# The 64-row and 32-row matmuls of two heads take turns, one by one, instead of head after head

## The chip, the cores and the metric

The kernel runs on one core of a Trainium2 chip. The metric is the device time of one launch in microseconds; three runs of the kernel before took 4888.07, 4894.80 and 4915.18 us, and their median, 4894.8 us, is the time before.

## What is computed

Two inputs of 1024 tokens by 1024 channels (a prompt and a sample) each go through two encoder layers, so there are four units of work. A layer is an input projection, four mixers side by side, and an output projection:

```
h = rms_norm(x, g_pre) * (1 + scale) + shift
proj = h @ w_in                                # 1024 x 1024 by 1024 x 3800
o_a = mla_mixer(...)                           # softmax attention, 4 heads
o_b = rwkv7_mixer(...)                         # linear attention with decay, 2 directions, 4 heads
o_c = mamba2_mixer(...)                        # state space, 2 directions
o_d = gated_deltanet_mixer(...)                # delta rule, 2 directions, 4 heads
x + gate * rms_norm(concat(o_a, o_b, o_c, o_d) @ w_out, g_post)
```

Mixers B and D are recurrences over the tokens. They are worked in 16 chunks of 64 tokens. Within a chunk a unit triangular 64 x 64 system is solved; between chunks a 64 x 64 state per head is carried. All of it is fp32.

## The kernel before

**Two heads lie in the two halves of the partitions.** A head has 64 channels and a chunk has 64 tokens, so in mixers B and D one head of a pair stands in partitions 0 to 63 and the other in 64 to 127. The code calls the half `x` (or `h`), the pair `pr`, and `half(x)` is the slice of 64 partitions. A matmul of one head reads 64 partitions and writes 64 partitions of PSUM, so it uses one 64 x 64 quarter of the TensorE array; a 32 x 32 matmul uses one sixteenth. Every fp32 matmul stands in the trace as two weight loads and two matmul records.

**Chunk matrices of mixer B** (`rwkv_dir`, lines 814 to 828). For each of 2 halves, 2 pairs and 16 chunks, two matmuls (`a` = 0, 1) read the rows of half `x` and write the two halves of PSUM in turn (line 824). Four chunks fill a bank of 512 columns; three banks (`b2p`) take turns. VectorE evicts a bank in four instructions (line 828). The loop over `x` is the outermost.

**Inverses** (`invert`, `merge`, lines 515 to 559). VectorE inverts the 32 x 32 diagonal blocks; `merge` joins them into 64 x 64 inverses with two rounds of 32 x 32 matmuls, for two groups `g` of 16 chunks. The round on line 551 fills one bank for each half `h`, ScalarE copies it to `Qs` (line 552), the round on line 558 multiplies `Qs` again, and VectorE copies the result (line 559). For each half there are 16 matmuls and then the half's copy. Three banks take turns, two a round. `merge` runs 16 times: 4 units, 2 mixers, 2 directions.

**The chains** (`rwkv_chain`, `gdn_chain`). 16 chunks in order, each a few small matmuls with VectorE and ScalarE between them (lines 905, 915, 928, 931 in B; 1195, 1207, 1220 in D). Those loops already have the half `x` innermost. Once for two chunks `batch` prepares the next pair: in B it loads `UV` by two DMAs, one for each half, then 8 matmuls (line 863) and 8 flips by the identity (line 565, called from 866) fill one PSUM tile `w`, ScalarE copies it, and 8 matmuls (line 875) fill another; in D it is 8 matmuls (line 1177). In all three the loop over `x` is the outermost. There are 64 batches of each mixer (4 units, 2 directions, 8 pairs of chunks).

**The order of the work.** A unit's mixers run in two streams (D then A; B then C) beside the projections of the neighbouring units: `in_tile` and `out_tiles` issue bulk 128 x 128 matmuls on line 458 through `paced`, whose groups of 5 or 8 are released by a memset on GpSimd (line 462). A planner writes every engine's queue ahead of time from the priorities given in the program: `urgent` puts `merge`, the chains and the weight splits (lines 327 and 329) ahead of the bulk. On the chip each engine then takes its queue in that fixed order, and an instruction that waits for a semaphore holds what is queued behind it.

Of the kernel before, what the change touches and what calls it, by code (L numbers as in the profile page):

```python
# [18 lines left out]
DRAM = bass.MemoryType.DRAM  # L19
MUL, ADD, SUB = ALU.mult, ALU.add, ALU.subtract  # L20

D = 1024
# [86 lines left out]
class Body:  # L109
# [22 lines left out]
    def open_io(self, ctx):  # L132
        """the pools of the projections"""
        self.pj = self.pool(ctx, "pj")
        self.sp = self.pool(ctx, "sp", 2)
        self.pps = self.pool(ctx, "pps", 2, PSUM)
# [20 lines left out]
    def sumsq(self, ps, col, sq, n, rhs, w, start=True, stop=True):  # L157
        """ps[:, col:col+w] = per-token sums over the channels of sq[:, 128 n : 128 n + 128]"""
        for x in range(2):
            self.nc.tensor.matmul(ps[64 * x:64 * x + 64, col:col + w], sq[:, n * 128 + 64 * x:n * 128 + 64 * x + 64], rhs,  # L160
                                  start=start, stop=stop)
# [99 lines left out]
    def stage_in(self, s, L, l, xsrc, Pd, parts=((0, W_ORDER), (1, W_ORDER))):  # L261
        """parts: (token half, tiles); the half of the part before is still there"""
        for hf, names in parts:
            if self.held is None or self.held[0] != (Pd, hf):
                self.spread()
                hh = self.t(self.pj, [128, 8, 512], F32R, tag="hh")
                hl = self.t(self.pj, [128, 8, 512], F32R, tag="hl")
                self.norm_in(s, L, xsrc, hf, hh, hl)
                self.held = (Pd, hf), hh, hl
            for name in names:  # L270
                self.spread()
                self.in_tile(l, name, hf, *self.held[1:], Pd)
# [59 lines left out]
    def out_tiles(self, l, ch, hh, hl, kqs, at=lambda kq: kq):  # L332
        """products of 4 token tiles with a quarter of the columns of w_out, over the quarters kqs of its rows"""
        nc, pj = self.nc, self.pj
        pss = [self.t(self.pps, [128, 2, 256], tag="pj") for _ in range(2)]
        for n, kq in enumerate(kqs):
            w = self.t(pj, [128, 2, 256], tag="w", bufs=2)
            self.dma(w, self.A["w_out"][l, ch, kq // 2][:, (kq % 2) * 512:(kq % 2) * 512 + 512].rearrange("p (k c) -> p k c", k=2))
            with self.urgent():
                wh, wl = self.split_w(w, [128, 2, 256])  # L340
            for i in range(4):
                ps = pss[i // 2][:, i % 2]
                c = slice(i * 128, (i + 1) * 128)
                for k in range(2):
                    a, b = hh[:, at(kq) * 2 + k, c], hl[:, at(kq) * 2 + k, c]
                    first, last = n == 0 and k == 0 and i % 2 == 0, n == len(kqs) - 1 and k == 1
                    for m, (u, w2) in enumerate(((a, wh), (a, wl), (b, wh))):
                        self.paced(TO, ps, u, w2[:, k], dict(start=first and m == 0, stop=last and m == 2, skip_group_check=True))
        return pss
# [50 lines left out]
    def stage_out_last(self, s, L, l, xsrc, od, dst, parts, ctx=None):  # L400
        """the last output in parts (token half, quarters of the rows of w_out, whether the sums begin or end),
        while the mixers of the later quarters still run"""
# [53 lines left out]
    def paced(self, n, *mm):  # L456
        """a matmul of a bulk stream: groups of n, each issued after the group before has begun"""
        m = self.nc.tensor.matmul(*mm[:3], **mm[3]).ins  # L458
        if self.gate is not None:
            self.tc.add_manual_dep(m, self.gate[0], SYNC, reason="pace")  # L460
        if self.run == 0:
            t = self.nc.gpsimd.memset(self.token, 0.0).ins  # L462
            self.tc.add_manual_dep(t, m.name, SYNC, reason="pace")
            self.next = t.name
        self.run += 1
        if self.run == n:
            self.gate, self.run = (self.next,), 0

# [10 lines left out]
    def behind(self, p0, p1, n, fs):  # L479
        """emit fs with priorities spread over those from p0 to p1"""  # L480
        keep = self.tc.cur_priority
        self.span, self.step = (p0, p1, n), 0
        for f in fs:
            f()
        self.span = None
        self.tc.cur_priority = max(keep, p1)
# [28 lines left out]
    def invert(self, pool, r, d, src):  # L515
        """r = inverses of the unit triangular 32 x 32 diagonal blocks of src, transposed"""
# [15 lines left out]
    def merge(self, pool, psp, r, d, src, dst):  # L532
        """dst = inverse of the unit triangular 64 x 64 blocks of src from the inverses r of their diagonal blocks"""
# [9 lines left out]
        for g in range(2):  # L543
            gs = slice(g * 16, g * 16 + 16)
            Qs = self.t(pool, [128, 16, 32], tag="mQ")
            p1 = [self.t(psp, [128, 512], tag="b") for _ in range(2)]
            for h in range(2):
                pa, pb = 64 * h + a, 64 * h + b
                A, B = slice(pa, pa + 32), slice(pb, pb + 32)
                for i in range(16):  # L550
                    nc.tensor.matmul(p1[h][B, i * 32:i * 32 + 32], src[h][a:a + 32, g * 16 + i, b:b + 32], Tr[A, g * 16 + i, :], start=True, stop=True, tile_position=(pa, pb))  # L551
                nc.scalar.copy(Qs[B].rearrange("p i t -> p (i t)"), p1[h][B])
            p2 = [self.t(psp, [128, 512], tag="b") for _ in range(2)]
            for h in range(2):
                pa, pb = 64 * h + a, 64 * h + b
                A, B = slice(pa, pa + 32), slice(pb, pb + 32)
                for i in range(16):
                    nc.tensor.matmul(p2[h][A, i * 32:i * 32 + 32], Qs[B, i, :], dst[h][b:b + 32, g * 16 + i, b:b + 32], start=True, stop=True, tile_position=(pb, pa))  # L558
                nc.vector.tensor_copy(dst[h][a:a + 32, gs, b:b + 32], p2[h][A].rearrange("p (i t) -> p i t", t=32))
# [7 lines left out]
    def pair_t(self, psp, dst, src, scale=None):  # L567
        """dst[(c parity, t), (c // 2, x, e)] = transposes of 8 chunks of both heads of src, times scale[(c parity, t), c // 2, x]"""
# [9 lines left out]
    def dma_pair(self, dst, src, swap):  # L578
        """dst[(x or 1 - x, t), c, e] (DRAM) = src[(c parity, t), (c // 2, x, e)]"""
# [6 lines left out]
    def head_sum(self, ps, sq, n):  # L586
        """ps[half, i] = sums over the channels of the head of the other half"""
# [4 lines left out]
    def heads_back(self, psp, y):  # L592
        """transposes back to channels: y[(1 - x, t), c, pr, e] -> [(pr, e), x, c, t]"""
# [5 lines left out]
    def rows2(self, t, r0, q):  # L599
        """rows r0 to r0 + 256 and quarter q of the tokens"""  # L600
# [55 lines left out]
    def rwkv_norm(self, p, psp, L, Pd, q, y, yd, bon, od, free):  # L656
        """normalisation, bonus and gate of a quarter of the tokens"""
# [29 lines left out]
    def rwkv_dir(self, L, Pd, l, d, yds, bons, od):  # L687
        nc, v = self.nc, self.nc.vector
        yd, bon = yds[d], bons[d]
        with ExitStack() as c0:  # L690
# [124 lines left out]
            with ExitStack() as c1:  # L815
                psp = self.pool(c1, "b2p", 3, PSUM)
                for x in range(2):
                    for pr in range(2):
                        for c4 in range(4):
                            ps = self.bank(psp)  # L820
                            for i in range(4):
                                c = c4 * 4 + i
                                for a in range(2):
                                    nc.tensor.matmul(ps[self.half(x ^ a), i * 128:i * 128 + 128], BK[self.half(x), pr, c, a],  # L824
                                                     AR[self.half(x), pr, c].rearrange("p a t -> p (a t)"), start=True, stop=True)
                            for i in range(4):
                                c = c4 * 4 + i
                                v.scalar_tensor_tensor(G[:, x, pr, c, :], ps[:, i * 128:i * 128 + 128], Dk[:, c, 2 * x + pr:2 * x + pr + 1], mk, MUL, MUL)  # L828
# [17 lines left out]
    def rwkv_chain(self, p, psp, d, AR, G, PL, Dk, vd, bkd, yd, pn, finish):  # L846
# [4 lines left out]
        def batch(j):  # L851
# [8 lines left out]
            for x in X:  # L860
                for pr in X:
                    for i in X:
                        nc.tensor.matmul(ps[half(1 - x), (pr * 2 + i) * 64:(pr * 2 + i) * 64 + 64], G[half(x), x, pr, 2 * j + i, 0:64], UV[half(x), x, pr, i, :],  # L863
                                         start=True, stop=True)
                        o = 256 + (pr * 2 + i) * 64
# [6 lines left out]
            for x in X:  # L872
                for pr in X:
                    for i in X:
# [199 lines left out]
    def gdn_norm(self, p, psp, L, Pd, q, y, yd, fq, od, free):  # L1074
        """normalisation and gate of a quarter of the tokens"""
# [70 lines left out]
    def gdn_chain(self, p, psp, d, GT, SC, kvd, be, kds, neg, el, yd, pn, finish):  # L1146
# [16 lines left out]
        def batch(j):  # L1163
# [10 lines left out]
            for x in X:  # L1174
                for pr in X:
                    for i in X:
# [321 lines left out]
    def attend(self, p, psp, qd, kd, krd, VO, ot):  # L1498
        """softmax of every head; the maxima of a head are found during the head before"""
# [74 lines left out]
    def mixers(self, L, Pd, l, od, which="dcab"):  # L1574
        """the streams right (d, a) and left (b, c)"""
# [9 lines left out]
    def last_mixers(self, L, Pd, l, od, io):  # L1585
        """three streams: d, c on the right; b; a in the place of the projections"""
# [16 lines left out]
    def full(self):  # L1603
# [32 lines left out]
        def ahead(w, n, f):  # L1636
            """emit f with priorities spread over the next w, n steps"""
# [87 lines left out]
```

## Time and profile before

| | |
|---|---|
| median of three runs | 4894.8 us |
| span of the profiled execution | 4894.9 us |
| PE (TensorE matmul) busy | 4389.3 us, 90% |
| DVE (VectorE) busy | 3343.1 us, 68% |
| ACT (ScalarE) busy | 2178.9 us, 45% |
| POOL (GpSimd) busy | 397.6 us, 8% |
| mean granted TensorE clock | 0.878 of full speed |

The span runs from the first to the last instruction; with one core there is nothing around it that the time would hold besides, and the two differ by 0.1 us. A busy time is the union of an engine's instructions. Matmul records last longer than the spacing of their starts, since matmuls are pipelined; what a run of matmuls costs is read from the start of its first to the start of the next thing behind it.

### The profile page before, as it was taken

To read this page: it belongs to the slowest core of one execution; us is meant where nothing else is said; L and a number is where in the kernel's file an instruction comes from. 1 tells how busy PE (TensorE), PEld (TensorE's weight loads), DVE (VectorE), ACT (ScalarE), POOL (GpSimd) and SP (SyncE) were. 2 spreads that over 40 slices of the span, in tenths; PEclk is the share of its full clock that TensorE was granted. 3 is DMA by queue.
4 is the path that set the end of the run, shared out by engine and by line. 5 is a ranking of instruction groups with operands and counts; after the bars stand their busy time and mean duration, and the time that the engine had idled before them with its cause. 6 is when DMAs were issued, how large, how long until landed. Compare 5 with 4: busy or idle time off the path is not lost.

```text
span 4894.9 us, 100724 instructions
## 1 busy us (share of the span) xinstructions
PE 4389.3 (90%) x38644; PEld 3358.2 (69%) x38644; DVE 3343.1 (68%) x6837; ACT 2178.9 (45%) x4734; POOL 397.6 (8%) x2093
## 2 busy tenths in 40 slices
PE   6879798999997988999989898899989989898997
PEld 3667576766776776756767667776767766776686
DVE  2488877566578787566459778657546968856666
ACT  2444363563434534443454453455344354344333
POOL 0101010000101000000011100000011100000001
PEclk8889898998997987989989798798889979878788
DMA  4444264242453546363345353545145535455224
GB/s 144 136 148 138 99 192 132 87 131 99 135 171 126 160 127 192 109 197 110 112 154 162 109 174 117 174 139 147 63 133 165 163 111 158 130 181 156 85 86 137
DMA packets 495063, 671.79 MB, mean 137 GB/s; under 512 B 149752, under 2 KB 265976, under 8 KB 493560
## 3 DMA queue, kind: packets, MB, share of 16 engines
q1 hardware_dynamic: 494584, 665.36, 43.6%
q8 instruction: 306, 5.01, 0.4%
q14 instruction: 173, 1.42, 0.1%
HBM read 486.53 MB, written 178.57 MB: 136 GB/s over the span
## 4 chain that ended last, share of the span: by engine, by line
PE 49%; DVE 13%; DMA 10%; issue 3%; ACT 3%; SPq 1%; POOL 0%; DVEq 0%; POOLq 0%; ACTq 0%
PE pj L458 21%; PE b L824 3%; PE b L1568 2%; PE b L551 2%; DVE iA L522 1%; PE b L558 1%; SPq L144 1%; PE b L1456 1%; PE b L1555 1%; PE pj L243 1%; PE w L863 1%; DVE wl L329 1%; DVE GT L537 1%; PE b L1524 1%; PE y L1220 1%
## 5 line engine op out<-in xcount | busy, mean ns | idle before, releaser
L458 PE MATMUL pj<-hh,wl 128*128 128x512 f32 (+1 forms) x2048 | 848.2, 415 | 32.0 <-DVE wl L329 18.4
L458 PE MATMUL pj<-hh,wh 128*128 128x512 f32 (+1 forms) x2048 | 854.6, 418 | 11.9 <-DVE iT L529 3.2
L458 PE MATMUL pj<-hl,wh 128*128 128x512 f32 (+1 forms) x2048 | 849.7, 415 | 16.9 <-POOL token L462 16.6
L327 ACT CAST wh<-w 128x512 fp32r<-128x512 f32 x640 | 395.1, 618 | 775.4 <-PE pj L458 495.1
L329 DVE TENSOR_TENSOR wl<-w,wh 128x512 fp32r<-128x512 f32 x640 | 446.6, 699 | 245.3 <-ACT wh L327 211.8
L458 PEld LDWEIGHTS pj<-hh,wl 128*128 128x128 f32 (+1 forms) x2048 | 397.5, 194 | 137.5 <-issue 20.7
L458 PEld LDWEIGHTS pj<-hh,wh 128*128 128x128 f32 (+1 forms) x2048 | 397.6, 194 | 115.3 <-issue 19.9
L458 PEld LDWEIGHTS pj<-hl,wh 128*128 128x128 f32 (+1 forms) x2048 | 396.9, 194 | 113.0 <-POOL token L462 22.9
L462 POOL MEMSET token<- 1x1 f32 x1613 | 143.7, 89 | 3317.1 <-PE pj L458 3307.1
L458 PE MATMUL pj<-wh,hl 128*128 128x256 f32 x896 | 266.6, 310 | 0.7 <-DVE hl L363 0.5
L458 PE MATMUL pj<-wh,hh 128*128 128x256 f32 x768 | 238.7, 311 | 6.3 <-ACT hh L362 4.1
L1559 ACT ACTIVATE pT<-b 128x512 f32<-128x512 f32 x256 | 149.8, 596 | 210.6 <-PE b L1557 207.4
L458 PE MATMUL pj<-wl,hh 128*128 128x256 f32 x768 | 234.0, 305 | 0.0
L294 PE MATMUL pj<-c_ident,x 128*128 128x128 f32 x416 | 118.8, 388 | 109.9 <-ACT hh L298 41.0
L1525 DVE TENSOR_REDUCE mx<-b 128x1 f32<-128x512 f32 x256 | 169.7, 686 | 68.5 <-PE b L1524 66.8
L638 DVE SCALAR_TENSOR_TENSOR cva<-cvi,cw,cva 128x1024 f32<-128x1024 f32 x144 | 183.9, 1279 | 47.4 <-ACT cva L634 29.3
L458 PEld LDWEIGHTS pj<-wh,hl 128*128 128x128 f32 x896 | 181.3, 207 | 14.2 <-issue 6.2
L296 ACT ACTIVATE ht<-pj,shc,gsc 128x256 f32<-128x256 f32 x208 | 118.4, 569 | 156.6 <-PE pj L294 84.0
L828 DVE SCALAR_TENSOR_TENSOR G<-b,Dk,mk 128x128 f32<-128x128 f32 x512 | 143.8, 344 | 61.9 <-PE b L824 61.1
L1568 PEld LDWEIGHTS b<-VO,pT 128*64 128x64 f32 x4096 | 150.2, 151 | 42.6 <-issue 29.4
L824 PE MATMUL b<-AR,BK 64*64 64x128 f32 x2048 | 176.7, 299 | 0.0
L1568 PE MATMUL b<-VO,pT 128*64 128x65 f32 x4096 | 168.4, 238 | 4.7 <-ACT pT L1559 4.3
(403 smaller groups left out, 9407.1 us busy)
## 6 DMA issues: line engine op xcount, KB each, us to landing
w<-w_in SPq DMA_DIRECT2D x512, 256.0 KB
P<-st SPq DMA_DIRECT2D x248, 256.0 KB
x<-x SPq DMA_DIRECT2D x76, 512.0 KB
w<-w_out SPq DMA_DIRECT2D x128, 256.0 KB
G<-P SPq DMA_DIRECT2D x112, 256.5 KB
cvi<-P SPq DMA_DIRECT2D x48, 512.0 KB
f<-acr SPq DMA_DIRECT2D x32, 512.0 KB
bkc<-bkd SPq DMA_DIRECT2D x64, 256.0 KB
```

Source lines behind the costliest of these rows:

```text
L294: nc.tensor.transpose(ps[:, i * 128:(i + 1) * 128], xs[i][:, k * 128:(k + 1) * 128], self.ident)
L296: nc.scalar.activation(ht, ps[:, 0:256], AF.Identity, scale=L.gsc[:, k, s:s + 1], bias=L.shc[:, k, s:s + 1])
L327: nc.scalar.copy(wh, w)
L329: nc.vector.tensor_tensor(wl, w, wh.bitcast(F32), SUB)
L458: m = self.nc.tensor.matmul(*mm[:3], **mm[3]).ins
L462: t = self.nc.gpsimd.memset(self.token, 0.0).ins
L638: nc.vector.scalar_tensor_tensor(a, c[:, j:j + 1024], wt(j, i), a, MUL, ADD)
L824: nc.tensor.matmul(ps[self.half(x ^ a), i * 128:i * 128 + 128], BK[self.half(x), pr, c, a], AR[self.half(x), pr, c].rearrange("p a t -> p ...
L828: v.scalar_tensor_tensor(G[:, x, pr, c, :], ps[:, i * 128:i * 128 + 128], Dk[:, c, 2 * x + pr:2 * x + pr + 1], mk, MUL, MUL)
L1525: v.tensor_reduce(mx[:, n, qt:qt + 1], ps, AX.X, ALU.max, negate=True)
L1559: nc.scalar.activation(pT[kt], ps, AF.Exp)
L1568: nc.tensor.matmul(po[64 * x:64 * x + 64, i, :], pT[kt][:, o:o + 64], VO[:, kt, h, :], start=(kt == 0 and i == 0), stop=(kt == 7), skip_gr ...
```

## The change

Four places get the half of the partitions as their innermost loop. In `rwkv_dir` a pair of banks, one for each half, is filled together and evicted afterwards. In `merge` both halves' 32 matmuls are issued in turn, and both copies come after them, in both rounds. In the three `batch` loops nothing but the order of the matmuls changes. The number of instructions, their shapes, operands and targets stay the same. (Elsewhere the diff only drops comments.)

```
@@ merge
-            for h in range(2):
-                pa, pb = 64 * h + a, 64 * h + b
-                A, B = slice(pa, pa + 32), slice(pb, pb + 32)
-                for i in range(16):
-                    nc.tensor.matmul(p1[h][B, i * 32:i * 32 + 32], src[h][a:a + 32, g * 16 + i, b:b + 32], Tr[A, g * 16 + i, :], start=True, stop=True, tile_position=(pa, pb))
+            at = [(64 * h + a, 64 * h + b) for h in range(2)]
+            AB = [(slice(pa, pa + 32), slice(pb, pb + 32)) for pa, pb in at]
+            for i in range(16):
+                for h, (A, B) in enumerate(AB):
+                    nc.tensor.matmul(p1[h][B, i * 32:i * 32 + 32], src[h][a:a + 32, g * 16 + i, b:b + 32], Tr[A, g * 16 + i, :], start=True, stop=True, tile_position=at[h])
+            for h, (A, B) in enumerate(AB):
                 nc.scalar.copy(Qs[B].rearrange("p i t -> p (i t)"), p1[h][B])
...
+            for i in range(16):
+                for h, (A, B) in enumerate(AB):
+                    nc.tensor.matmul(p2[h][A, i * 32:i * 32 + 32], Qs[B, i, :], dst[h][b:b + 32, g * 16 + i, b:b + 32], start=True, stop=True, tile_position=at[h][::-1])
+            for h, (A, B) in enumerate(AB):
                 nc.vector.tensor_copy(dst[h][a:a + 32, gs, b:b + 32], p2[h][A].rearrange("p (i t) -> p i t", t=32))
@@ rwkv_dir
-                for x in range(2):
-                    for pr in range(2):
-                        for c4 in range(4):
-                            ps = self.bank(psp)
...
+                for pr in range(2):
+                    for c4 in range(4):
+                        pss = [self.bank(psp) for _ in range(2)]
+                        for i in range(4):
+                            c = c4 * 4 + i
+                            for a in range(2):
+                                for x in range(2):
+                                    nc.tensor.matmul(pss[x][self.half(x ^ a), i * 128:i * 128 + 128], BK[self.half(x), pr, c, a],
+                                                     AR[self.half(x), pr, c].rearrange("p a t -> p (a t)"), start=True, stop=True)
+                        for x in range(2):
                             for i in range(4):
                                 c = c4 * 4 + i
...
+                                v.scalar_tensor_tensor(G[:, x, pr, c, :], pss[x][:, i * 128:i * 128 + 128], Dk[:, c, 2 * x + pr:2 * x + pr + 1], mk, MUL, MUL)
@@ rwkv_chain, batch
-            for x in X:
-                for pr in X:
-                    for i in X:
+            for pr in X:
+                for i in X:
+                    for x in X:
                         nc.tensor.matmul(ps[half(1 - x), (pr * 2 + i) * 64:(pr * 2 + i) * 64 + 64], G[half(x), x, pr, 2 * j + i, 0:64], UV[half(x), x, pr, i, :],
                                          start=True, stop=True)
+                    for x in X:
                         o = 256 + (pr * 2 + i) * 64
                         self.flip(ps[half(1 - x), o:o + 64], AR[half(x), pr, 2 * j + i, 0, :], half(x))
@@ the same turn of the loops (pr, i, x for x, pr, i) at line 875 of rwkv_chain and at line 1177 of gdn_chain
```

## Rows read from the trace of the kernel before

**Rows 1.** The page: busy times, and the chain of waits by engine.

```profile
PE 4389.3 (90%) x38644; PEld 3358.2 (69%) x38644; DVE 3343.1 (68%) x6837; ACT 2178.9 (45%) x4734; POOL 397.6 (8%) x2093
PE 49%; DVE 13%; DMA 10%; issue 3%; ACT 3%; SPq 1%; POOL 0%; DVEq 0%; POOLq 0%; ACTq 0%
```

**Rows 2.** Span and mean granted TensorE clock.

```profile
core 0: 4894.9 us, clock 0.878
```

**Rows 3.** Groups by line: operands, count, busy us, mean ns, idle before and releasers.

```profile
L824 PE MATMUL b<-AR,BK 64*64 64x128 f32 x2048 | 176.7, 299 | 0.0
...
L863 PE MATMUL w<-UV,G 64*64 64x64 f32 x1024 | 132.9, 240 | 5.6 <-DMA UV<-vd 5.0 <-DVE qf L1516 0.3 <-PE us L905 0.3
...
L552 ACT COPY mQ<-b 32x512 f32<-32x512 f32 x64 | 36.9, 576 | 228.0 <-PE b L551 228.0
...
L559 DVE COPY G<-b 32x512 f32<-32x512 f32 x32 | 22.0, 687 | 48.3 <-PE b L558 48.2
```

**Rows 4.** Timeline of a batch of B and what follows (start us, us, instruction, records).

```profile
871.58 0.32 PE L863 MATMUL w<-UV,G 64*64 64x64 f32 x2
...
873.20 0.28 PE L565 MATMUL w<-c_ident,AR 64*64 64x64 f32 x2
873.41 0.33 PE L931 MATMUL y<-UV,G 128*64 128x64 f32 x2
...
877.49 0.96 PE L875 MATMUL w<-G,At 64*64 64x64 f32 x16
878.38 0.50 PE L1524 MATMUL b<-kh,qh 96*128 96x512 f32 x1
```

**Rows 5.** Timeline of a batch of D and what follows.

```profile
434.41 0.96 PE L1177 MATMUL w<-GT,SC 64*64 64x64 f32 x16
435.30 0.50 PE L458 MATMUL pj<-hl,wh 128*128 128x512 f32 x1
```

**Rows 6.** Timeline of two runs whose halves already take turns, same stretch.

```profile
879.52 0.45 PE L905 MATMUL us<-ZS,G 128*64 128x64 f32 x8
879.90 0.44 PE L928 MATMUL y<-ZS,AR 64*64 64x64 f32 x6
880.27 0.50 PE L1524 MATMUL b<-kh,qh 96*128 96x512 f32 x1
```

**Rows 7.** Timeline of a merge alone on PE.

```profile
1897.98 3.68 PE L551 MATMUL b<-mT,G 32*32 32x32 f32 x61 [5.61 <-DVE mT L542]
...
1901.47 0.24 PE L551 MATMUL b<-mT,G 32*32 32x32 f32 x1
1901.50 0.24 PE L558 MATMUL b<-G,mQ 32*32 32x32 f32 x1
...
1910.87 0.58 PE L458 MATMUL pj<-wh,hh 128*128 128x256 f32 x1
```

**Rows 8.** Timeline of a merge at full clock, one run.

```profile
3484.50 2.01 PE L558 MATMUL b<-G,mQ 32*32 32x32 f32 x61
```

**Rows 9.** Two merges' stretches: busy us of PE, PEld, DVE, ACT, POOL; granted clock; DMA.

```profile
1898.00:1912.00 14.00, 13.98 (x261) 13.78 (x262) 10.66 (x17) 3.98 (x6) 2.10 (x4) 0.50 0.58 189
3096.90:3117.50 20.60, 20.60 (x312) 19.55 (x313) 10.42 (x19) 5.83 (x14) 0.79 (x7) 0.67 0.34 112
```

**Rows 10.** Timeline of chunk matrices, and of a run that turns both rows and columns.

```profile
737.62 1.96 PE L824 MATMUL b<-AR,BK 64*64 64x128 f32 x32
...
262.67 2.87 PE L1064 MATMUL b<-KQ 64*64 64x128 f32 x46
```

**Rows 11.** Timeline of the eviction of one bank of chunk matrices on VectorE.

```profile
742.04 1.13 DVE L828 SCALAR_TENSOR_TENSOR G<-b,Dk,mk 128x128 f32<-128x128 f32 x4 [0.18 <-PE b L824]
```

**Rows 12.** Two stretches of chunk matrices, same columns as rows 9.

```profile
735.40:761.50 26.10, 26.10 (x321) 20.48 (x321) 22.41 (x77) 2.79 (x6) 3.12 (x9) 1.00 0.27 89
2971.00:3007.70 36.70, 36.70 (x481) 30.54 (x480) 30.33 (x93) 10.61 (x31) 0.98 (x7) 0.84 0.33 104
```

**Rows 13.** Timeline of SP's queue: issue of the two loads of UV.

```profile
884.88 1.18 SPq L144 DMA_DIRECT2D UV<-vd  x2
```

More of the change, by code (lines that the diff above doesn't have):

```diff
@@ L546, in merge @@
             p1 = [self.t(psp, [128, 512], tag="b") for _ in range(2)]
-            for h in range(2):
-                pa, pb = 64 * h + a, 64 * h + b
-                A, B = slice(pa, pa + 32), slice(pb, pb + 32)
-                for i in range(16):
-                    nc.tensor.matmul(p1[h][B, i * 32:i * 32 + 32], src[h][a:a + 32, g * 16 + i, b:b + 32], Tr[A, g * 16 + i, :], start=True, stop=True, tile_position=(pa, pb))
+            at = [(64 * h + a, 64 * h + b) for h in range(2)]
[4 more added lines that the diff above has]
+            for h, (A, B) in enumerate(AB):
                 nc.scalar.copy(Qs[B].rearrange("p i t -> p (i t)"), p1[h][B])
             p2 = [self.t(psp, [128, 512], tag="b") for _ in range(2)]
[L554 to L558, printed above, removed]
+            for i in range(16):
+                for h, (A, B) in enumerate(AB):
+                    nc.tensor.matmul(p2[h][A, i * 32:i * 32 + 32], Qs[B, i, :], dst[h][b:b + 32, g * 16 + i, b:b + 32], start=True, stop=True, tile_position=at[h][::-1])
+            for h, (A, B) in enumerate(AB):
                 nc.vector.tensor_copy(dst[h][a:a + 32, gs, b:b + 32], p2[h][A].rearrange("p (i t) -> p i t", t=32))
@@ L816, in rwkv_dir @@
                 psp = self.pool(c1, "b2p", 3, PSUM)
-                for x in range(2):
-                    for pr in range(2):
-                        for c4 in range(4):
-                            ps = self.bank(psp)
+                for pr in range(2):
[8 more added lines that the diff above has]
+                        for x in range(2):
                             for i in range(4):
                                 c = c4 * 4 + i
[L823 to L828, printed above, removed]
+                                v.scalar_tensor_tensor(G[:, x, pr, c, :], pss[x][:, i * 128:i * 128 + 128], Dk[:, c, 2 * x + pr:2 * x + pr + 1], mk, MUL, MUL)
             cB.close()
@@ L871, in batch @@
             ps = self.t(psp, [128, 512], tag="w")
-            for x in X:
-                for pr in X:
-                    for i in X:
+            for pr in X:
+                for i in X:
+                    for x in X:
                         nc.tensor.matmul(ps[half(x), (pr * 2 + i) * 64:(pr * 2 + i) * 64 + 64], At[half(1 - x), pr, i, :], G[half(1 - x), x, pr, 2 * j + i, 0:64],
@@ L1173, in batch @@
             ps = self.t(psp, [128, 512], tag="w")
-            for x in X:
-                for pr in X:
-                    for i in X:
+            for pr in X:
+                for i in X:
+                    for x in X:
                         nc.tensor.matmul(ps[half(x), (pr * 2 + i) * 64:(pr * 2 + i) * 64 + 64], kn[half(1 - x), pr, i, :], GT[half(1 - x), x, pr, 2 * j + i, 0, :],
```

## The prediction

> **What bounds the kernel now.** I read the page's busy times first: TensorE is at work for 4389.3 of 4894.9 us, far more than VectorE's 3343.1 [rows 1]. The profiled execution stands at the median of the runs (4894.9 against 4894.8), so its span can be used as it is [rows 2]. The chain of waits tempers that: its PE share is 49% of the span, with 13% VectorE and 10% DMA between [rows 1]. So TensorE is the bound, but only 49 of its 90 points lie on the path that sets the end; I carry a saved microsecond of TensorE to the end at 49/90 = 0.54, and at 0.9 (its busy share) in the best case. The groups by line give the operands and counts of the lines touched; the rest is read from timelines, because there a run of matmuls has a price: from its start to the start of what stands behind it.
>
> **The rate of one array tile, and of two.** A batch of B holds 16 matmuls, 32 records, and takes 871.58 to 873.41, 1.83 us, 57 ns a record [rows 4]; all of one half use one tile of the array. Where the halves already take turns, 8 records go from 879.52 to 879.90, 0.38 us [rows 6]. With 0.24 us for one record [rows 3] inside the 0.45 us of that run, 7 steps take 0.21 us: 30 ns a record and 0.14 us at the ends. Two tiles thus run side by side, each at its old rate, and that is the whole effect of the change: where one tile was busy, two will be.
>
> **Batches.** 1.83 us becomes 0.14 + 32 x 0.030 = 1.10, so 0.73 us goes, 64 times: 47 us. The runs on line 875 (877.49 to 878.38, 0.89 us for 16 records [rows 4]) and line 1177 (434.41 to 435.30, also 0.89 us [rows 5]) become 0.14 + 16 x 0.030 = 0.62; 0.27 us, 128 times: 35 us. Nothing is added to any queue. One wait moves: the second matmul now reads the second half of `UV`. SP issues both loads in 1.18 us [rows 13], so it may come 0.6 us later, and formerly eight matmuls and eight flips of the first half covered that. At 64 batches this is 0 to 38 us; TensorE stood 5.0 us in all for `UV` in the whole run [rows 3], so the loads are mostly long there, and I take 5 us. Behind the waiting matmul stands the bulk stream, in the same queue.
>
> The Trainium skill ("TensorEngine Tiling (Array Packing)", "Gotcha 1: PSUM Pressure") says that different row tiles cannot use one PSUM bank at the same time. Both halves of a batch write one bank, so by that rule these 82 us would be nothing. Lines 905 and 928 write both halves into one bank too, 928 from different rows, and stay at 0.45 us for 8 and 0.44 us for 6 records [rows 6]; by that row I keep the 82 us and hold the rule as a rival.
>
> **Merges.** A merge alone takes 1897.98 to 1910.87, 12.9 us for 256 records, 50 ns each [rows 7], at half the clock (0.50 in that stretch, TensorE busy for 14.0 of its 14.0 us [rows 9]) after 5.61 us of standing [rows 7]. Where the end of one round overlaps the next, records of the two lines start 27 to 30 ns apart (1901.47, 1901.50) [rows 7]: two tiles, half the price. Taking turns, a round of 64 records costs 64 x 0.027 = 1.7 us, four of them 6.9. But a cover goes. Today ScalarE copies half 0 while half 1 is multiplied, and TensorE never stands in that merge. Now both copies follow the round: 0.24 us for the last record and 2 x 0.576 [rows 3] = 1.4 us, twice; and before round 3 the first VectorE copy, 0.24 + 0.687 [rows 3] = 0.9 us, because the three banks are then short by one. That is 3.7 us, so 10.6 with nothing in the gaps, and 0.69 for the second copy at the end: 1.6 us gained; 6.0 if bulk matmuls fill the gaps. A part of the merges is warmer (0.67 in one stretch [rows 9]); at full clock one tile gives (2.01 - 0.24) / 60 = 30 ns a record [rows 8], which makes 7.7 us before and, even at 15 ns, 3.9 + 3.7 + 0.7 = 8.3 after: a loss of 0.6 unfilled. Over 16 merges the bounds are 18 us (12 cold at 1.6, 4 warm at a small loss) and 16 x 6.0 = 96. Merges go ahead of the bulk, which the planner may put into known gaps; I take the middle, 60 us.
>
> **Chunk matrices.** Here two tiles already work: the two `a` write different columns. 32 records take 1.96 us [rows 10], (1.96 - 0.30) / 31 = 54 ns; a run that turns both rows and columns, still two tiles, has (2.87 - 0.30) / 45 = 57 [rows 10]. The change sets four tiles going; no row shows four. Bounds: 54 to 27 ns over 2048 records [rows 3], 55 us gained; or no gain and a new wait. A pair needs two banks of three, so its second matmul waits until VectorE has evicted one, 1.13 us [rows 11], with the bulk queued behind; 64 pairs make 72 us lost. In the stretch nearest to pure, TensorE is busy all 26.1 us and VectorE 22.4 of them [rows 12]: when TensorE gets cheap, VectorE is late next, 3.7 us lower. Eight stages: 30 us, which I take.
>
> **The sum.** 47 + 35 - 5 + 60 + 30 = 167 us of TensorE. At 0.54 it is 90 us: 4895 - 90 = 4805 us. Ends for this case, the merges from 18 to 96 and the chunk matrices from 0 to 55: 95 to 228, at 0.54 51 and 123, or 4772 to 4844.
>
> **Rivals.** (1) TensorE is the bound throughout and each microsecond counts: 47 + 35 + 96 + 55 = 233, at 0.9 210 us: 4685. For it: 90% busy. Against: 49% of the chain. (2) Two halves in one bank don't overlap: the batches give nothing, 167 - 82 = 85, at 0.54 46: 4849. Rows 6 speak against it. (3) The lost covers are paid in full: 82 gained in the batches, 38 lost on `UV`, 18 gained in the merges, 72 lost on banks, together 10 lost: 4900, no change. For it: a fixed queue, in which a waiting matmul holds the bulk. Against: the planner knows these waits and can put ready bulk before them.
> (4) Slower, by the clock. The mean grant is 0.878 [rows 2]; merges get 0.50 while TensorE is busy throughout [rows 9], chunk matrices 1.00 and 0.84 [rows 12]. If short dense bursts with waits between them bring other stages to the merges' level, each 0.01 of the mean costs 4389 x 0.01 / 0.878 = 50 us of TensorE. At 0.845 the 167 us are gone; from there on it decides, and at 0.82 the loss is 290 - 167 = 123, at 0.54 66 us: 4961. For it: the merges' own rows. Against: a stretch of chunk matrices, which already run two tiles in such bursts, holds 1.00 [rows 12].
>
> **How the numbers follow.** The forecast case has 0.48, rival 1 0.17, rival 2 0.07, rival 3 0.15, rival 4 0.13. Less than 0.5%, 24 us, can't be told from no change here. Faster is the forecast with rivals 1 and 2: 0.72; no change is rival 3: 0.15; slower rival 4: 0.13. The range reaches into rival 1 as far as 4700 and past rival 3 to 4925; what is left out is the better half of rival 1 and nearly all of rival 4, 0.2 together.
>
> **What would show it.** Right: the 32 records of a batch in about 1.1 us and the 16 of lines 875 and 1177 in about 0.6; merges near 27 ns a record with gaps of about 1.4 us, in which bulk stands or nothing; chunk matrices under 40 ns a record; PE busy down by some 150 us. Wrong: pairs of halves that start as far apart as before (rival 2); TensorE's idle time up by as much as its busy time falls, with line 552's and 828's engines as releasers (rival 3); a mean grant under 0.85 (rival 4). If a merge's clock rose by itself, or if the planner laid the bulk out quite differently, the sum would rest on the wrong rows.

## The result, and the profile after

The changed kernel takes 4839.35 us in the median of 11 runs, the kernel before 4894.8: a ratio of 0.9897 (95% interval 0.9870 to 0.9923), 50 us less by the ratio. The forecast was 4805, with 4700 to 4925 around it. The sign and the range held; the experiments show that the working under them held for one of its three parts (batches, merges, chunk matrices), and that the 50 us can't be laid to the turns from this one comparison.

The page of the changed kernel, to be set beside [rows 1]: span, engines (busy, share of the span, instructions) and the shares of the chain that ended last:

```profile
span 4862.1 us, 100716 instructions
PE 4303.3 (89%) x38644; PEld 3243.0 (67%) x38644; DVE 3351.1 (69%) x6837; ACT 2177.4 (45%) x4734; POOL 399.5 (8%) x2093
PE 58%; DVE 16%; DMA 14%; issue 5%; ACT 5%; SPq 1%; POOL 1%; DVEq 0%; POOLq 0%; ACTq 0%
```

Its span and granted clock, beside [rows 2]:

```profile
core 0: 4862.1 us, clock 0.877
```

TensorE is busy for 86 us less, not 167, and the span is 33 us shorter: the time in which it is not busy (span less busy) rose from 505.6 to 558.8 us. The chain's shares add up to 100% here; the ones of [rows 1] to 79%: that chain was followed back only to some 1000 us after the span's start, and 49% was too low a share to read a conversion from.

The groups by line (as [rows 3]; line 864 was 863, 877 was 875, 1179 was 1177, 557 was 558):

```profile
L824 PE MATMUL b<-AR,BK 64*64 64x128 f32 x2048 | 178.4, 305 | 3.5 <-DVE G L829 3.2
L864 PE MATMUL w<-UV,G 64*64 64x64 f32 x1024 | 89.2, 248 | 14.6 <-DMA UV<-vd 7.8 <-issue 6.0 <-PE us L907 0.6
...
L551 PE MATMUL b<-mT,SC 32*32 32x32 f32 x1024 | 56.4, 230 | 32.5 <-DVE mT L542 29.4 <-ACT mQ L553 3.0
```

Line 863's busy time fell from 132.9 to 89.2 us; line 824's did not fall at all (176.7 to 178.4). The merges' first round, line 551, is still held up mostly by VectorE's transposes (line 542, 29.4 us). Summed from each record's start to the next one's (at most its own end), the batches went from 261.1 to 177.9 us, the merges from 208.4 to 188.4, the chunk matrices from 161.9 to 159.9.

Of the 53 us of added idle time 46 stand before the bulk matmuls of line 458 (79 us before the change, 126 after, all its groups together). One of these groups, before and after; most of its wait is for the weights that VectorE splits (`wl`, line 329):

```profile
L458 PE MATMUL pj<-hh,wl 128*128 128x512 f32 (+1 forms) x2048 | 848.2, 415 | 32.0 <-DVE wl L329 18.4
...
L458 PE MATMUL pj<-hh,wl 128*128 128x512 f32 (+1 forms) x2048 | 849.4, 415 | 41.9 <-DVE wl L329 28.8 <-POOL token L462 13.1
```

Timeline of a run on line 1179 and of one on line 877, and what follows each, as [rows 4, 5] (start in us, length, engine, line, records):

```profile
433.31 0.68 PE L1179 MATMUL w<-GT,SC 64*64 64x64 f32 x16
433.93 0.50 PE L458 MATMUL pj<-hl,wh 128*128 128x512 f32 x1
...
849.21 0.68 PE L877 MATMUL w<-G,At 64*64 64x64 f32 x16
849.82 0.50 PE L458 MATMUL pj<-hh,wh 128*128 128x512 f32 x1
```

From its start to the next line's, 16 records take 0.62 and 0.61 us where they took 0.89: the step of the prediction, to a hundredth. The merge tells another story (timeline, as [rows 7]):

```profile
407.16 1.91 PE L551 MATMUL b<-mT,SC 32*32 32x32 f32 x32 [0.61 <-DVE mT L542]
409.00 0.80 PE L458 MATMUL pj<-hh,wh 128*128 128x512 f32 x1
...
410.15 1.75 PE L551 MATMUL b<-mT,SC 32*32 32x32 f32 x29
...
411.85 3.09 PE L557 MATMUL b<-GT,mQ 32*32 32x32 f32 x58
```

32 records in 1.91 us are 54 ns each (the last one's own 0.24 us taken off, 31 starts in 1.67), one tile's price at the lower clock (0.50 in that stretch, as in the merge of [rows 7]): nothing takes turns. TensorE's queue, as the planner wrote it, says so too (entry, line, output and inputs, number of matmuls in a row). For this merge it is the same as before, entry for entry:

```
1022 L551 MATMUL b_874_4412<-mT_872_4408,SC_864_4314 32x32 x16
1023 L458 MATMUL pj_492_2326<-hh_322_1500,wh_494_2329 128x512
1024 L458 MATMUL pj_492_2326<-hl_323_1501,wh_494_2329 128x512
1025 L551 MATMUL b_875_4413<-mT_872_4408,SC_864_4314 32x32 x16
1026 L557 MATMUL b_876_4448<-GT_869_4393,mQ_873_4411 32x32 x16
1027 L557 MATMUL b_877_4449<-GT_869_4393,mQ_873_4411 32x32 x16
```

In the changed kernel 784 of the 1024 matmuls on line 551 and 560 of those on line 557 stand 16 in a row, 328 of 1024 chunk matrices 8 in a row (504 in the kernel before, where the planner already mixed banks without being asked). The order in the program is only a wish. The likely reason, which no run tests by itself: one half's operands are there before the other's, since its transposes (line 542) and copies (line 553) come first, or its bank is free while the other's is not, and the planner issues what is ready. In the batches both halves write one PSUM tile and become ready together, and the turns stand as written.

Where chunk matrices do take turns, four tiles work (timeline, both at full clock):

```profile
736.37 1.09 PE L824 MATMUL b<-AR,BK 64*64 64x128 f32 x16
...
4142.88 1.10 PE L824 MATMUL b<-AR,BK 64*64 64x128 f32 x30
```

One bank's 16 records take 1.09 us, 30 records in turns 1.10: about 28 ns a record instead of 53.

### The profile page after: what moved, and what is told of

Its sections match the earlier page's. It is cut to its first block, busy times and chain, and to the rows that moved or that the text cites. A ratio compares the mean times of both kernels' runs of the same rounds, so it can differ in the third digit from the quotient of the medians.

```text
span 4862.1 us, 100716 instructions
## 1 busy us (share of the span) xinstructions
PE 4303.3 (89%) x38644; PEld 3243.0 (67%) x38644; DVE 3351.1 (69%) x6837; ACT 2177.4 (45%) x4734; POOL 399.5 (8%) x2093
## 4 chain that ended last, share of the span: by engine, by line
PE 58%; DVE 16%; DMA 14%; issue 5%; ACT 5%; SPq 1%; POOL 1%; DVEq 0%; POOLq 0%; ACTq 0%
PE pj L458 27%; PE b L824 2%; DVE iA L522 2%; PE b L1570 2%; PE b L551 2%; DMA w<-w_in 2%; PE pj L243 2%; PE b L557 1%; PE b L1557 1%; DVE wl L329 1%; DVE GT L537 1%; SPq L144 1%; PE y L1222 1%; PE b L1526 1%; PE b L590 1%
## 5 line engine op out<-in xcount | busy, mean ns | idle before, releaser
L458 PEld LDWEIGHTS pj<-hh,wh 128*128 128x128 f32 (+1 forms) x2048 | 398.0, 194 | 128.8 <-POOL token L462 16.1
L1570 PE MATMUL b<-VO,pT 128*64 128x65 f32 x4096 | 182.5, 233 | 0.9 <-ACT pT L1561 0.9
L824 PE MATMUL b<-AR,BK 64*64 64x128 f32 x2048 | 178.4, 305 | 3.5 <-DVE G L829 3.2
```

Of the source, the lines that this page charges most:

```text
L824: nc.tensor.matmul(pss[x][self.half(x ^ a), i * 128:i * 128 + 128], BK[self.half(x), pr, c, a], AR[self.half(x), pr, c].rearrange("p a t - ...
L1570: nc.tensor.matmul(po[64 * x:64 * x + 64, i, :], pT[kt][:, o:o + 64], VO[:, kt, h, :], start=(kt == 0 and i == 0), stop=(kt == 7), skip_gr ...
```

## The experiments

Ratios are to the kernel before on the same chip.

**Batches alone, and the rest alone.** The two halves of the diff, each put back into the other kernel.

> Changed kernel with merge and the chunk matrices as before; only the batch loops (lines 863/565, 875, 1177) take turns. Theory A (the whole gain is the batches, because only there the queue on TensorE really alternates): ratio to the kernel before 0.987 to 0.993, TensorE time from start to start on these lines down by about 80 us as in the changed kernel. Theory B (merge and chunk matrices carry a good part, 90 of the 167 us of the sum): ratio 0.994 to 0.998.

Measured: 1.0002 (0.9969 to 1.0035). The batches took 177.6 us, as in the changed kernel, yet the time did not move. Theory A misses; so does B, though the interval reaches into its range. The page and the clock of this run:

```profile
PE 4342.5 (89%) x38644; PEld 3286.9 (67%) x38644; DVE 3348.9 (68%) x6837; ACT 2174.2 (44%) x4734; POOL 396.5 (8%) x2093
```

```profile
core 0: 4894.1 us, clock 0.882
```

TensorE's busy time fell by 47 us, not by the 83 that the batches lost: other lines took longer, the untouched chunk matrices 186.0 instead of 161.9 us. And what fell came back as time in which it is not busy (551.6 instead of 505.6 us).

> Kernel before with only merge and the chunk matrices changed; batches as before. Theory A: ratio 0.996 to 1.002; most rounds of a merge still stand in the queue as 16 matmuls of one half and then 16 of the other. Theory B: 0.990 to 0.995. Theory C (the gain is an accident of a newly planned queue, whatever is turned): about 0.99 as well.

Measured: 1.0083 (1.0040 to 1.0125), slower, though the merges' and chunk matrices' own time fell by 33 us; it lies outside the ranges of all three theories. Two parts at 1.0002 and 1.0083 that together give 0.9897 don't add up: something else than the turned matmuls moves the time by more than a per cent.

**Another queue for the same work.** Three kernels without any turns. One swaps two loops around the chunk matrices, two set a constant of the bulk work's priorities to 1810 or 1790:

```
-                for x in range(2):
-                    for pr in range(2):
+                for pr in range(2):
+                    for x in range(2):
                         for c4 in range(4):
...
-MIX = 1800
+MIX = 1810
```

> Kernel before, only the chunk-matrix loops run pair outside half (pr, x, c4 for x, pr, c4): nothing takes turns, the same matmuls, but the planner writes another queue from entry 1885 of 14508 on. Theory P (a newly planned queue alone moves the time by up to 1%): TensorE start-to-start time within 20 us of before, ratio anywhere from 0.99 to 1.01, clear of 1. Rival (the plan is neutral, so that ratios near 0.99 or 1.008 come from the turning): 0.998 to 1.002.

Measured: 0.9917 (0.9891 to 0.9943).

> Kernel before with the constant 1800, over which the early bulk work's priorities are spread, at 1810: nothing takes turns, the queue differs from entry 805 on. Theory P: 0.99 to 1.01, clear of 1; rival: 0.998 to 1.002.

Measured: 0.9920 (0.9888 to 0.9952).

> Kernel before with the constant at 1790, nothing in turns: a third plan of the same work. Theory P: 0.99 to 1.01, TensorE time within 40 us of before.

Measured: 1.0259 (1.0224 to 1.0294). Theory P holds for the time, and was too narrow: the same matmuls in another queue spread over 3.4% of it. On TensorE's own time it misses: busy time moved by -42 us with the swapped loops and by +144 at 1790, where 20 and 40 were the most expected. The page of the run at 1790, and its span and granted clock:

```profile
span 5040.3 us, 100664 instructions
PE 4533.2 (90%) x38644; PEld 3450.1 (68%) x38644; DVE 3350.3 (66%) x6837; ACT 2182.1 (43%) x4734; POOL 401.4 (8%) x2093
```

```profile
core 0: 5040.3 us, clock 0.859
```

The same two views of the swapped loops:

```profile
PE 4347.1 (89%) x38644; PEld 3332.9 (69%) x38644; DVE 3355.2 (69%) x6837; ACT 2175.4 (45%) x4734; POOL 399.4 (8%) x2093
```

```profile
core 0: 4858.7 us, clock 0.888
```

And of the run at 1810:

```profile
PE 4390.4 (90%) x38644; PEld 3364.0 (69%) x38644; DVE 3349.4 (68%) x6837; ACT 2181.5 (45%) x4734; POOL 399.2 (8%) x2093
```

```profile
core 0: 4898.7 us, clock 0.881
```

The time outside busy (span less busy) is the same within 6 us in all four plans, the kernel before, 1790, swapped loops and 1810: 505.6, 507.1, 511.6 and 508.3 us (5040.3 - 4533.2, 4858.7 - 4347.1, 4898.7 - 4390.4). The whole difference is busy time of the same 38644 records, and it goes with the granted clock: 0.859, 0.878, 0.881 and 0.888 with 5040, 4895, 4899 and 4859 us, some 60 us for each 0.01. The grant is not all of it: between executions of one and the same kernel, the one before, 0.01 goes with 36 to 42 us (a line through each of its three sets of 11, 17 and 24 executions beside the experiments). In the traces 7512 of TensorE's records start at the lower of its two levels (1.2 GHz) with the swapped loops, 9387 at 1790; priced with what each shape takes from start to start at either level, these make some 130 of the 186 us of busy time between the two, an estimate. The other 56 us belong to the order in some other way that no run singles out. Why one queue is granted more than another is open.

**The batches in two more plans.**

> The same with the batches in turns. If the batches' 83 us of TensorE count as in the prediction (0.54): 0.009 below the run without turns, on average over plans; if they count for nothing, as in the run with the batches alone: equal on average, with the spread of the plans on top.

Measured: 0.9888 (0.9855 to 0.9922), 0.003 below its partner.

> The same with the batches in turns: 0.009 below the run without turns on average if the batches count at 0.54, equal on average if they don't.

Measured: 0.9971 (0.9940 to 1.0002), 0.005 above its partner. With the first pair (0.000) and the changed kernel against the one without turned batches (0.9897 - 1.0083 = -0.019), the four differences average -0.004, with a standard deviation of 0.010: the batches' share isn't settled. Steadier is what becomes of the saved time. The time outside busy rises in every pair: 505.6 to 551.6, 511.6 to 550.7, 508.3 to 538.3, 532.3 to 558.8 us, 35 on average. Set against the 83 us saved in the batches, two fifths come back as waiting.

**Turns that the planner has to keep.** Each matmul of a round is ordered behind the one before in the queue, without a wait:

```
+    def turn(self, prev, m):
+        if prev is not None:
+            self.tc.add_manual_dep(m.ins, prev.ins.name, NOSYNC, reason="turn")
+        return m
...
-                    nc.tensor.matmul(p1[h][B, ...
+                    last = self.turn(last, nc.tensor.matmul(p1[h][B, ...
```

> Changed kernel with each matmul of a pair of chunk-matrix banks ordered behind the one before (order in the queue only, no wait), so that all 1024 alternate. If the array runs four tiles side by side: 27 to 30 ns a record at full clock in the whole line, 162 us of this line's start-to-start time down to about 100, and with the bank wait (VectorE 1.13 us a bank) as standing time behind it; ratio 0.984 to 0.992. If the lost cover decides (rival 3): TensorE stands 30 to 70 us more than in the changed kernel and the ratio is 0.99 to 1.0.

Measured: 0.9882 (0.9843 to 0.9921). The line's start-to-start time fell to 128.7 us, not 100; TensorE was outside busy for 605.0 us, 46 more than in the changed kernel, as rival 3 has it. The ratio lies in the first theory's range, but beside the changed kernel's 0.9897 no gain in time is seen.

> Changed kernel with each matmul of a merge round ordered behind the one before, so that all 2048 alternate. Two tiles: 27 ns a record at half clock, 16 to 18 at full clock, lines 551 and 558 together from 188 us to 100 to 120. If that time counts as in the prediction: 40 us less, ratio 0.980 to 0.986. If the copies that no longer run beside the other half (1.4 us twice a merge, 0.9 once) and the later second half decide: merges as long as in the changed kernel, 17 to 21 us, and a ratio of 0.987 to 0.995.

Measured: 0.9938 (0.9908 to 0.9968). Timeline of a forced merge (lines 553 and 560 are the two rounds, 555 the copies):

```profile
409.54 1.91 PE L553 MATMUL b<-mT,SC 32*32 32x32 f32 x62 [1.06 <-DVE mT L543]
411.40 1.18 ACT L555 COPY mQ<-b 32x512 f32<-32x512 f32 x2 [4.40 <-PE b L553]
412.03 0.31 PE L560 MATMUL b<-GT,mQ 32*32 32x32 f32 x2 [0.57 <-ACT mQ L555]
412.63 1.75 PE L560 MATMUL b<-GT,mQ 32*32 32x32 f32 x57 [0.29 <-ACT mQ L555]
...
422.89 1.19 PE L553 MATMUL b<-mT,SC 32*32 32x32 f32 x62
424.01 0.50 PE L459 MATMUL pj<-hh,wh 128*128 128x512 f32 x1
```

The rates are those of the prediction: 62 records in 1.91 us are 27 ns, at full clock 1.19 us, 16 ns. The lost covers are there too: after the first of these rounds TensorE waits for the copies (0.57 and 0.29 us); after the second, bulk matmuls (line 459) stand in the gap. All merges together took 108.8 us instead of 188.4, and TensorE was outside busy for 611.1 us, 52 more than in the changed kernel; a merge lasts 17.9 us on average, 19.1 in the kernels before and after. So the second theory came: most of what the turns save there is waited away.

**The largest dose, in three plans.**

> Everything in turns and ordered so in the queue: batches, all chunk matrices, all merge rounds. The largest dose: TensorE start-to-start time about 200 us below the kernel before (83 batches, 90 merges, 33 chunk matrices). If a saved microsecond counts 0.54: 108 us, ratio 0.978. If two fifths or more come back as waiting and the rest counts: TensorE stands 80 to 120 us more, ratio 0.983 to 0.990. If the span follows something else: 0.99 to 1.0.

Measured: 0.9784 (0.9761 to 0.9806).

> The same with the constant at 1810, to be set against the run at 1810 without turns (0.992): 0.970 at 0.54, 0.976 to 0.983 if two fifths come back as waiting, about 0.992 if it counts for nothing; a plan of its own may add or take up to 0.01.

Measured: 0.9881 (0.9861 to 0.9902).

> Everything in turns and ordered so, constant at 1790: 0.022 below the run at 1790 without turns at 0.54, 0.010 to 0.017 below if two fifths come back as waiting, equal if it counts for nothing.

Measured: 0.9699 (0.9675 to 0.9722), 4747.31 us: it beats both kernels. Its page, its span and granted clock, and its groups of the three lines:

```profile
PE 4123.5 (87%) x38644; PEld 3096.0 (65%) x38644; DVE 3337.2 (70%) x6837; ACT 2175.3 (46%) x4734; POOL 397.5 (8%) x2093
```

```profile
core 0: 4737.0 us, clock 0.894
```

```profile
L834 PE MATMUL b<-AR,BK 64*64 64x128 f32 x2048 | 131.3, 302 | 22.9 <-DVE G L839 21.3 <-DVE Dk L797 1.6
L553 PE MATMUL b<-mT,SC 32*32 32x32 f32 x1024 | 31.7, 223 | 46.1 <-DVE mT L543 45.0 <-DVE GT L562 1.1
L560 PE MATMUL b<-GT,mQ 32*32 32x32 f32 x1024 | 28.8, 220 | 6.3 <-ACT mQ L555 6.2
```

Against the plan without turns at the same constant the three differ by -0.022, -0.004 and -0.056, -0.027 on average; the expected figures are met in the first plan (0.978, with 0.54), in the second nearly nothing came, and in the third more than any of them. In all three plans it is faster, and all three lie below all four plans without turns (0.9699 to 0.9881 against 0.9917 to 1.0259), so the turns are worth something; by how much is drowned by the plans. The time outside busy is 654.3, 664.1 and 613.5 us, 106 to 156 more than without turns; the rows name VectorE for 21.3 us of it, which frees the banks of line 834 late. The other two pages, at 1800 and 1810:

```profile
PE 4154.1 (86%) x38644; PEld 3112.3 (65%) x38644; DVE 3339.2 (69%) x6837; ACT 2176.0 (45%) x4734; POOL 396.6 (8%) x2093
...
PE 4161.0 (86%) x38644; PEld 3121.3 (65%) x38644; DVE 3338.7 (69%) x6837; ACT 2176.6 (45%) x4734; POOL 396.5 (8%) x2093
```

In these two the fall of busy time is almost all the turned lines' own (start to start 229 of 235 us, and 221 of 229), and 149 and 156 us of it come back as time outside busy: 0.37 and 0.32 of a saved microsecond are left in the span. At 1790 the turned lines account for only 272 of 410 us; there the grant rose from 0.859 to 0.894 as well.

## Why the prediction was right, and where it was not

**The rate, and the batches: right.** 82 us were worked out and 83.2 measured. Two halves in one PSUM bank, each in its own partitions, do run side by side (0.61 us for 16 records), so rival 2 falls. By the sentence of the Trainium skill ("TensorEngine Tiling (Array Packing)", "Gotcha 1: PSUM Pressure") that different row tiles cannot use one PSUM bank at the same time, these turns would have saved nothing; here the measurement decides. The wait for `UV` was taken as 5 us: the idle time before line 863's matmuls rose by 9.0 us, from 5.6 to 14.6, of which the rows lay 7.8 to `UV` and 6.0 to nothing that the profile shows.

**The merges: 60 us were put in, 20 came.** The term was mis-sized because the order in the program was taken for the order in the queue, where 784 and 560 of 1024 matmuls still stand 16 in a row. The price of two tiles was right wherever they were made to work (27 ns at the lower clock, 16 at the full one).

**The chunk matrices: 30 put in, 2 came,** in part for the same reason. But the 2 are no measure of the turns: in the four plans without turns the line takes between 160.6 and 193.2 us. Kept in turns it takes 117.1 to 128.8, and four tiles do give 28 ns a record.

**What the saved time is worth: 0.54 was not shown.** It came from a chain that was followed only in part. 86 us of busy time and 33 us of span in the profiles make 0.38, the two forced plans 0.37 and 0.32. That 0.54 x 86 = 46 comes near the measured 50 is no proof, since a plan alone moved the time by anything from -41 to +127 us: that the measured time fell into the range is in good part luck.

**Rival 3** (lost covers) is seen where the turns are forced, and takes a part, not all. **Rival 4**, slower by the clock, did not come: 0.877 after 0.878. But its lever is real: in kernels without any turns the plan alone moved the grant between 0.859 and 0.888, and some 60 us go with each 0.01 between plans, 36 to 42 between executions of one kernel, where 50 were worked out. **Rival 1** is out: in every pair a part of what the batches save, 27 to 46 us, comes back as waiting.

## What to carry to other kernels

Where a planner writes the queues, read the queue and not the loop nest: turns that the program asks for were kept here where both halves become ready at once, and elsewhere an order-only edge kept them, at the price of waiting for the later half. Before a per cent is laid to an edit, run two or three plans of the same work, here a swapped loop or a nudged constant, and see how far they spread. Price a saving on the busiest engine in two parts, the busy time that goes and the waiting that comes back.

## What was not expected of the hardware

Matmuls of different tiles need not start in the order of the queue. In the merge of [rows 7] the queue holds 32 matmuls of line 551 and then those of line 558, yet the first records of line 558 start before the last ones of line 551 (timeline):

```profile
1901.50 0.24 PE L558 MATMUL b<-G,mQ 32*32 32x32 f32 x1
1901.53 0.24 PE L551 MATMUL b<-mT,G 32*32 32x32 f32 x1
1901.55 0.24 PE L558 MATMUL b<-G,mQ 32*32 32x32 f32 x1
1901.58 0.24 PE L551 MATMUL b<-mT,G 32*32 32x32 f32 x1
```

32 x 32 matmuls that take turns on two tiles start 16 ns apart on average at full clock (62 records in 1.19 us). More than two tiles help as well: 64 x 64 ones start 28 ns apart on four tiles, half the price of two. The mean granted clock of one and the same work differs from queue to queue by 0.029, and 182 us of span go with it (4858.7 to 5040.3), while the time outside busy stays within 6 us.
